# A hybrid diffusion backbone on one core: pads in two tile pools, 64-byte shifts of some weight tiles, and another order inside the attention items

## The chip, the cores and the metric

The kernel runs on one core of one Trainium2 chip. The metric is the device time of one execution in microseconds (us); lower is better. The core has a matrix engine (TensorE, PE in the profile; its weight loads are listed as PEld), three engines for elementwise work (VectorE = DVE, ScalarE = ACT, GpSimd = POOL), and queues that start DMA transfers, of which this kernel uses mainly SP's and POOL's. The on-chip memory SBUF has 128 partitions; a tile occupies the same byte range in each of them, so a tile's place is one byte address. Products accumulate in PSUM.

## The reference

Two layers work on 1024 latent tokens (a 16 x 64 grid) and 256 context tokens of width 1024, in float32.

```python
# layer 0: FNet Fourier groups || bidirectional order-2 Hyena
p = u @ w_in                                   # (L, 2048)
y = concat([fourier_mix(p[..., :512]), hyena_mix(p[..., 512:], ...)]) @ w_out
# layer 1: 2-D neighbourhood attention, 16 heads of 64
s_loc = einsum("bcqhd,bicjhd->bhcqij", q_r, k_b) * scale + bias    # masked outside the window
s_ctx = einsum("bcqhd,bjhd->bhcqj", q_r, kc) * scale               # all 256 context keys
p = softmax(concat([s_loc, s_ctx]))
o = p_loc @ v_b + p_ctx @ vc ;  y = o @ w_out
# after each mixer
h = h + g1 * y
h = h + g2 * ((silu(m @ w_gate) * (m @ w_up)) @ w_down)            # m = modulated RMS norm of h
```

Shifts, scales and gates come from adaLN products of a conditioning vector; the context tokens share all weights, have their own modulation, and need no output in the last layer. The result is the final RMS norm of the latent tokens.

## The kernel before

**Precision and products.** Activations are held transposed, 128 channels on the partitions and tokens along the row. Float32 precision is had from the faster type float32r by splitting: a value is the sum of a high part (a rounded copy, made on ACT by line 280) and a low part (the difference, made on DVE by line 282), and a product is three matmuls, high x high, high x low and low x high. So most of the 16,320 matmuls have float32r operands and move 512 or 256 columns: 512 for each half of the latent tokens, 256 for the context.

**Pools of tiles.** A pool has a number of buffers for each tag, and the pools lie in SBUF in the order in which they are opened: constants (`cp`), wide tiles `s4` (20 of 4096 bytes), `s2` (35 of 2048), `g` (4 of 2048), `pt` (6 `t` tiles of 2048 bytes, and small statistics tiles `ah` and `st` of 32 and 64 bytes, 6 each), `tk` (4 of 2048), and `pw` with the tags `ws`, `wh` and `wl` (2 each of 4096). The profile prints `s4` and `s2` both as `s`. A weight block is loaded by DMA into `ws` (or a wide `s` tile) as float32 and split into `wh` and `wl`; matrices that come as float16 are loaded into `ws` (printed `cs`) and copied to a float32r tile `mat`, which takes buffers of `wh` and `wl` in turn. Activations lie in `s` tiles. In SBUF the last byte used before the change is 227,616 in each partition.

**Stages, in order of time.** Filter spectra of the Hyena branch (to about 210 us), the input projection with the Fourier channel side and the context's filters between its blocks (to about 500), the Hyena convolutions and the Fourier sequence side (to about 780), the output projection, the feed-forward block of layer 0 (context columns first, then gate and up of the latent tokens by a Strassen-Winograd scheme of seven products, line 1246, then down, line 1413, then the context's down, line 1516, to about 1690), the value projection (to about 1870), attention (to about 2330), the rest of the attention's output projection, and layer 1's feed-forward block.

**Roles of the tiles in a matmul.** In the input, output, key, query, gate and up products the weights (`wh`, `wl`) are the stationary operand and an `s` tile moves. In the filter spectra and the forward transforms of the Hyena branch `mat` is stationary. In the inverse Hyena transforms `mat` moves, 256 columns at a time; in the value projection `wh` and `wl` move, 512 at a time. In the later Strassen-Winograd products and in the latent down products both operands are `s` tiles (or `t`).

**Attention.** There are 64 items, one for each head, half of the rows, and pair of column chunks (`attn_item`). An item has three stages: (a) TensorE computes the context scores of both chunks into one PSUM tile and the local scores into two; (b) DVE takes the row maxima (line 1699 for the context, line 1701 for bias plus local scores of each chunk), their negation (1703), ACT takes the exponentials (1706 for the local scores in the `g` tile, 1707 for the context scores in `t`), each with a sum, TensorE transposes the three probability tiles through the identity (1715), ACT copies each to float16 (1718) and DVE makes the low half (1719); (c) TensorE multiplies with the values, and ACT scales the result (1745). Two items of neighbouring stages are in flight, and the key and query projections of the next pair of heads, and at the end the output projection's first part, are issued between the stages as filler.

**Order of the work.** Each engine has its own queue and executes it in order. The code is written in one order; a planner that estimates times then orders each engine's queue, so an edit can move instructions that it doesn't touch.

Of the kernel before, what the change touches and what calls it, by code (L numbers as in the profile page):

```python
# [18 lines left out]
P = 128  # L19
# [4 lines left out]
NFB = 22  # L24
# [6 lines left out]
KSTART = (0, 8, 24, 32)  # L31
BOPS = ("B11", "B21", "T2", "T1", "T3", "B22", "T4")
# [167 lines left out]
class Builder:  # L200
    def __init__(self, ctx, tc, a, out, taps=None, stop=None):
        self.tc, self.nc, self.a, self.out = tc, tc.nc, a, out
        self.taps, self.stop = taps, stop
        ent = ctx.enter_context
        self.cp = ent(tc.tile_pool(name="cp", bufs=1))
        self.p4 = ent(tc.tile_pool(name="p4", bufs=20))
        self.p2 = ent(tc.tile_pool(name="p2", bufs=35))
        self.pg = ent(tc.tile_pool(name="pg", bufs=4))
        self.pt = ent(tc.tile_pool(name="pt", bufs=6))
        self.pko = ent(tc.tile_pool(name="pk", bufs=4))  # L210
        self.pw = ent(tc.tile_pool(name="pw", bufs=2))
        self.pp = ent(tc.tile_pool(name="pp", bufs=6, space=bass.MemoryType.PSUM))
        self.pq = ent(tc.tile_pool(name="pq", bufs=2, space=bass.MemoryType.PSUM))
        self.dr = ent(tc.tile_pool(name="dr", bufs=1, space=bass.MemoryType.DRAM))
        self.k = self.mk = self.pk = 0
        self.banks = 8
        self.sq = {}

# [67 lines left out]

    def pair3(self):

        self.p3 = (getattr(self, "p3", 0) + 1) % 3
        return self.pair2(("ws", "ws") if self.p3 == 0 else ("wh", "wl"))  # L290

    def weights(self, src, w=1024, cut=False, keep=None, wide=False, load=None):
        st = self.S4() if wide else self.pw.tile([P, 1024], F32, tag="ws", name=self.nm("ws"))
        if keep:
            hi, lo = keep
        else:
            hi, lo = self.pair3() if wide == 3 else self.pair2()
        (load or self.ld)(st.rearrange("p (n k) -> p n k", n=4) if cut else st[:, :w], src)
        self.split(st[:, :w], hi[:, :w], lo[:, :w])
        return hi, lo  # L300
# [5 lines left out]
    def cmat(self, w, src, view=None, small=False):  # L306
# [8 lines left out]
        m = self.mat(w)  # L315
# [506 lines left out]
    def hy_inverse(self, sq, o, y):  # L822
# [8 lines left out]
        for h in range(H // hw):  # L831
# [25 lines left out]
            for part, fi, i, fb in mats:  # L857
                ms[(i, fb)] = self.cmat(min(nb, 2) * 512, a["vi_" + sq][h, i, :, fb:fb + min(nb, 2)],
                                        lambda t: t.rearrange("p (f c) -> p f c", c=512), False)
                if sq == "l":  # L860
                    for cb in range(4):
                        product(part, fi, i, fb, cb)
                    yield
# [427 lines left out]
    def ffn(self, l, u, h, hs, second, after, keep=None, begun={}):  # L1291
# [21 lines left out]
        todo = iter(())  # L1313
        if u is not None:
            for fb in range(NFB):
                wide = 3 if fb < NFB - 2 else True
# [77 lines left out]
    def down(self, l, bops, sops, hidc, hs, h, todo, after, keep):  # L1394
# [98 lines left out]
        if l == 0:  # L1493
# [4 lines left out]
            for kb in range(NFB):  # L1498
# [9 lines left out]
                wh, wl = self.pair2()  # L1508
# [165 lines left out]
    def attn_item(self, head, hd, hf, c0, qs, kk, kc, vt, osb, out):  # L1674
# [24 lines left out]
        nc.vector.tensor_reduce(cm, pctx.rearrange("p (i k) -> p i k", i=2), axis=AX, op=MAX)  # L1699
        for i in (0, 1):  # L1700
            nc.vector.tensor_tensor_reduce(bias[i], loc[i][:, :384], bias[i], 1.0, cm[:, i:i + 1], ADD, MAX,
                                           mx[:, i:i + 1])
        nc.vector.tensor_scalar(nm, mx, -1.0, None, op0=MUL)
        pc = self.T()
        for i in (0, 1):
            nc.scalar.activation(bias[i], bias[i], AF.Exp, bias=nm[:, i:i + 1], accum_out=s1[:, i:i + 1])
            nc.scalar.activation(pc[:, i * 256:i * 256 + 256], pctx[:, i * 256:i * 256 + 256], AF.Exp,
                                 bias=nm[:, i:i + 1], accum_out=s2[:, i:i + 1])
        nc.vector.tensor_tensor(s1, s1, s2, ADD)
        nc.vector.reciprocal(rv, s1)  # L1710
        pts = []
        for src, n in ((pc, 4), (bias[0], 3), (bias[1], 3)):
# [7 lines left out]
            pts.append(t)  # L1720
# [437 lines left out]
```

## Time and profile before

| | before |
|---|---|
| median of 3 runs | 3058.11 us (3051.83 to 3061.61) |
| profiled execution | 3055.81 us, of it span 3054.0 us |
| granted TensorE clock, mean | 0.985 |
| PE busy | 2919.6 us (96%), 16,320 matmuls |
| DVE busy | 2076.6 us (68%) |
| ACT busy | 1390.4 us (46%) |
| POOL busy | 460.3 us (15%) |
| DMA | 549.87 MB, mean 180 GB/s |

The span runs from the first to the last instruction; busy times are shares of it. A row of a group reads: line, engine, operation, output tile <- input tiles, shape, number of instructions, then busy time, mean time of one in ns, and the idle time of the engine ahead of them with what ended it. Matmuls are pipelined, so the mean of one is longer than the distance between two starts. A row of the timeline begins with the start and the duration in us of a merged run of instructions. A row of waits names who waited for whom, the total in us, how often, and the longest.

### The profile page before, as it was taken

What the parts mean: (1) busy time and instruction counts of PE and PEld (TensorE: products, weight loads), DVE (VectorE), ACT (ScalarE), POOL (GpSimd) and SP (SyncE); (2) the same over time, 40 slices, a digit from 0 to 9 for tenths busy, and PEclk for the clock granted to TensorE, in tenths of its full rate; (3) what the DMA queues carried; (4) which work ended last, traced back from release to release, by engine and by line L of the source; (5) the groups of instructions that cost most, each with busy time, mean ns of one, the idle gap of its engine ahead of it and who ended that gap; (6) DMA issues with size and microseconds to landing.
All of it is one profiled execution on the core that took longest, in us unless ns stands there. A gap on an engine that the chain in (4) does not pass through costs nothing. (4 is left out here: it accounts for less than half of the span.)

```text
span 3054.0 us, 45753 instructions
## 1 busy us (share of the span) xinstructions
PE 2919.6 (96%) x16320; PEld 2420.3 (79%) x16320; DVE 2076.6 (68%) x3924; ACT 1390.4 (46%) x2581; POOL 460.3 (15%) x751
## 2 busy tenths in 40 slices
PE   7899999999999999999999999999889999999997
PEld 2678888888899788787778888888777788887886
DVE  5767785775677777866677437777676977664545
ACT  4663225453454333333445336777675533333433
POOL 1012012451101111212010000110111022112000
PEclk9999999999999999999999999999999999999999
DMA  6564545466555454659874334454555266535663
GB/s 250 190 204 169 182 141 155 124 199 206 210 172 200 170 181 170 215 177 325 299 252 165 131 126 116 127 143 124 164 180 187 97 234 221 173 111 175 214 193 131
DMA packets 263486, 549.87 MB, mean 180 GB/s; under 512 B 33878, under 2 KB 85784, under 8 KB 263258
## 3 DMA queue, kind: packets, MB, share of 16 engines
q1 hardware_dynamic: 209658, 381.23, 38.5%
q0 software_dynamic: 51296, 161.52, 15.1%
q10 hardware_dynamic: 2304, 4.20, 0.4%
q8 instruction: 128, 2.10, 0.3%
q14 instruction: 100, 0.82, 0.1%
HBM read 418.63 MB, written 119.80 MB: 176 GB/s over the span
## 5 line engine op out<-in xcount | busy, mean ns | idle before, releaser
L1246 PE MATMUL ps<-s,s 128*128 128x512 f32 x2028 | 513.0, 395 | 14.3 <-ACT g L1251 11.0
L1246 PEld LDWEIGHTS ps<-s,s 128*128 128x128 f32 x2028 | 384.6, 190 | 103.4 <-ACT g L1251 13.4
L276 PE MATMUL ps<-s,wh 128*128 128x256 f32 (+1 forms) x1768 | 391.7, 327 | 1.3 <-ACT wh L280 1.3
L276 PEld LDWEIGHTS ps<-s,wh 128*128 128x128 f32 x1768 | 291.4, 188 | 37.2 <-ACT wh L280 3.4
L276 PE MATMUL pq<-s,wh 128*128 128x512 f32 (+1 forms) x984 | 300.9, 384 | 10.3 <-DVE s L1630 7.6
L280 ACT CAST wh<-ws 128x1024 fp32r<-128x1024 f32 (+1 forms) x139 | 142.6, 1026 | 351.2 <-PE ps L276 163.2
L1413 PE MATMUL ps<-s,s 128*128 128x512 f32 (+1 forms) x1000 | 258.6, 384 | 11.2 <-DVE s L282 11.0
L282 DVE TENSOR_TENSOR wl<-ws,wh 128x1024 fp32r<-128x1024 f32 (+1 forms) x139 | 165.7, 1192 | 142.2 <-ACT wh L280 137.3
L280 ACT CAST s<-s 128x1024 fp32r<-128x1024 f32 (+2 forms) x188 | 171.7, 942 | 197.9 <-DMA s<-d 160.1
L276 PE MATMUL ps<-s,wl 128*128 128x256 f32 (+1 forms) x884 | 255.1, 326 | 1.1 <-DVE wl L282 1.1
L276 PE MATMUL ps<-s,s 128*128 128x64 f16 (+3 forms) x2663 | 216.5, 233 | 16.2 <-DVE s L1719 5.9
L1413 PEld LDWEIGHTS ps<-s,s 128*128 128x128 f32 x1000 | 183.7, 188 | 53.0 <-DVE s L282 17.1
L282 DVE TENSOR_TENSOR s<-s,s 128x1024 fp32r<-128x1024 f32 (+2 forms) x166 | 190.7, 1184 | 45.4 <-ACT s L280 44.8
L280 ACT CAST s<-t 128x512 fp32r<-128x512 f32 (+2 forms) x250 | 140.4, 579 | 175.6 <-DVE t L1225 67.6
L276 PEld LDWEIGHTS pq<-s,wh 128*128 128x128 f32 x984 | 177.8, 190 | 45.9 <-DVE s L1630 9.9
L282 DVE TENSOR_TENSOR s<-t,s 128x512 fp32r<-128x512 f32 (+2 forms) x250 | 164.4, 671 | 58.6 <-ACT s L280 32.9
L1246 PE MATMUL ps<-s,wh 128*128 128x512 f32 x608 | 194.9, 398 | 2.0 <-DVE g L1337 2.0
L276 PE MATMUL ps<-s,mat 128*128 128x512 f32 x684 | 180.9, 410 | 6.2 <-ACT s L280 3.2
L276 PE MATMUL pq<-s,wl 128*128 128x512 f32 (+1 forms) x492 | 183.0, 381 | 0.0
L276 PEld LDWEIGHTS ps<-s,wl 128*128 128x128 f32 x884 | 162.1, 188 | 18.5 <-DVE wl L282 1.7
L316 ACT CAST mat<-cs 128x1024 fp32r<-128x1024 f16 (+2 forms) x120 | 111.7, 935 | 131.6 <-PE ps L276 52.4
L276 PEld LDWEIGHTS ps<-s,mat 128*128 128x128 f32 x684 | 132.0, 196 | 43.6 <-DVE s L282 5.4
(379 smaller groups left out, 5666.0 us busy)
## 6 DMA issues: line engine op xcount, KB each, us to landing
s<-d SPq DMA_DIRECT2D x286, 256.0 KB, 3.6
s<-in_down SPq DMA_DIRECT2D x154, 256.0 KB, 4.0
d<-s POOLq DMA_DIRECT2D x137, 256.0 KB, 3.6
d<-tk POOLq DMA_DIRECT2D x98, 256.0 KB, 3.7
s<-in_ada_w POOLq DMA_DIRECT2D x48, 512.0 KB, 4.7
g<-in_bias SPq DMA_DIRECT2D x128, 192.0 KB, 2.9
ws<-in_up SPq DMA_DIRECT2D x44, 512.0 KB, 3.5
d<-g POOLq DMA_DIRECT2D x87, 256.0 KB, 3.3
```

The lines of the kernel that those rows point to most:

```text
L276: self.nc.tensor.matmul(o, l, r, start=st, stop=sp)
L280: self.last_hi = nc.scalar.copy(hi, src).ins
L282: self.last_lo = eng.tensor_tensor(lo, src, hi.bitcast(F32), SUB).ins
L316: self.nc.scalar.copy(m, st)
L1246: nc.tensor.matmul(ps, x[:, sl], y, start=first and j == 0 and x is wh and y is xh, stop=j == 3 and x is wl, skip_group_check=True)
L1413: m = nc.tensor.matmul(acc[j][:, c0:c1], x[:, sl], y[:, xs], start=first and k == 0, stop=last and k == 2, skip_group_check=True)
```

## The change

Two pads are added: 72 float32 columns (288 bytes) in the constants' pool, and 112 columns (448 bytes) in `pt`; each is written once by a memset on POOL. A helper `shifted` takes a tile of 1056 columns in `wh`, `wl` or `ws` and hands out the part that begins 16 columns (64 bytes) in; the context's gate, up and down weights and the matrices of the inverse Hyena transforms (`cmat` with `shift`) are taken through it. The buffers of `wh`, `wl` and `ws` thereby grow from 4096 to 4224 bytes, and the last byte used is 229,120. In an attention item the negated maximum is taken separately for each chunk, right behind that chunk's maximum; the context exponential is issued ahead of the local one; and the transposes go in the order local chunk 0, context, local chunk 1, where the context had been first. In the built queues nothing else is moved ahead of attention or behind it; inside attention all queues have another order.

```diff
+PAD_C, PAD_T, SHIFT = 72, 112, 16
...
+        self.pad(self.cp, PAD_C)
...
+    def pad(self, pool, w):
+
+        self.nc.gpsimd.memset(pool.tile([P, w], F32, name="pad", tag="pad", bufs=1), 0.0)
...
+    def shifted(self, tag, name, w=1024):
+
+        return self.pw.tile([P, 1056], F32R, tag=tag, name=self.nm(name))[:, SHIFT:SHIFT + w]
+
+    def pair1(self):
+        return self.shifted("wh", "wh"), self.shifted("wl", "wl")
+
     def pair3(self):
 
         self.p3 = (getattr(self, "p3", 0) + 1) % 3
-        return self.pair2(("ws", "ws") if self.p3 == 0 else ("wh", "wl"))
+        tags = ("ws", "ws") if self.p3 == 0 else ("wh", "wl")
+        return [self.shifted(g, n) for g, n in zip(tags, ("wh", "wl"))]
...
-            hi, lo = self.pair3() if wide == 3 else self.pair2()
+            hi, lo = self.pair3() if wide == 3 else self.pair1() if wide == 2 else self.pair2()
...
-        m = self.mat(w)
+        if shift:
+            self.mk ^= 1
+            m = self.shifted(("wh", "wl")[self.mk], "mat", w)
+        else:
+            m = self.mat(w)
...
-                                        lambda t: t.rearrange("p (f c) -> p f c", c=512), False)
+                                        lambda t: t.rearrange("p (f c) -> p f c", c=512), False, True)
...
+        if l == 0:
+            self.pad(self.pt, PAD_T)
...
-                wide = 3 if fb < NFB - 2 else True
+                wide = 3 if fb < NFB - 2 else 2
...
-                wh, wl = self.pair2()
+                wh, wl = self.pair1()
...
         nc.vector.tensor_reduce(cm, pctx.rearrange("p (i k) -> p i k", i=2), axis=AX, op=MAX)
+        pc = self.T()
         for i in (0, 1):
             nc.vector.tensor_tensor_reduce(bias[i], loc[i][:, :384], bias[i], 1.0, cm[:, i:i + 1], ADD, MAX,
                                            mx[:, i:i + 1])
-        nc.vector.tensor_scalar(nm, mx, -1.0, None, op0=MUL)
-        pc = self.T()
-        for i in (0, 1):
-            nc.scalar.activation(bias[i], bias[i], AF.Exp, bias=nm[:, i:i + 1], accum_out=s1[:, i:i + 1])
+            nc.vector.tensor_scalar(nm[:, i:i + 1], mx[:, i:i + 1], -1.0, None, op0=MUL)
             nc.scalar.activation(pc[:, i * 256:i * 256 + 256], pctx[:, i * 256:i * 256 + 256], AF.Exp,
                                  bias=nm[:, i:i + 1], accum_out=s2[:, i:i + 1])
+            nc.scalar.activation(bias[i], bias[i], AF.Exp, bias=nm[:, i:i + 1], accum_out=s1[:, i:i + 1])
...
-        for src, n in ((pc, 4), (bias[0], 3), (bias[1], 3)):
+        for k, src, n in ((1, bias[0], 3), (0, pc, 4), (2, bias[1], 3)):
...
-            pts.append(t)
+            pts[k] = t
```

More of the change, by code (lines that the diff above doesn't have):

```diff
@@ L304, in mat, with cmat @@
         return self.pw.tile([P, w], dt, tag=("wh", "wl")[self.mk], name=self.nm("mat"))
-    def cmat(self, w, src, view=None, small=False):
+    def cmat(self, w, src, view=None, small=False, shift=False):
         if small:
@@ L1702, in attn_item @@
                                            mx[:, i:i + 1])
-        nc.vector.tensor_scalar(nm, mx, -1.0, None, op0=MUL)
-        pc = self.T()
-        for i in (0, 1):
-            nc.scalar.activation(bias[i], bias[i], AF.Exp, bias=nm[:, i:i + 1], accum_out=s1[:, i:i + 1])
+            nc.vector.tensor_scalar(nm[:, i:i + 1], mx[:, i:i + 1], -1.0, None, op0=MUL)
             nc.scalar.activation(pc[:, i * 256:i * 256 + 256], pctx[:, i * 256:i * 256 + 256], AF.Exp,
                                  bias=nm[:, i:i + 1], accum_out=s2[:, i:i + 1])
+            nc.scalar.activation(bias[i], bias[i], AF.Exp, bias=nm[:, i:i + 1], accum_out=s1[:, i:i + 1])
         nc.vector.tensor_tensor(s1, s1, s2, ADD)
         nc.vector.reciprocal(rv, s1)
-        pts = []
-        for src, n in ((pc, 4), (bias[0], 3), (bias[1], 3)):
+        pts = [None] * 3
+        for k, src, n in ((1, bias[0], 3), (0, pc, 4), (2, bias[1], 3)):
             ps = self.PS()
```

## Prediction

> **What bounds the kernel now.** I read the page first, then busy time by stage, then the timeline of TensorE inside long back-to-back runs, and last the waits of the attention stage.
>
> ```profile
> span 3054.0 us, 45753 instructions
> ...
> PE 2919.6 (96%) x16320; PEld 2420.3 (79%) x16320; DVE 2076.6 (68%) x3924; ACT 1390.4 (46%) x2581; POOL 460.3 (15%) x751
> ...
> PEclk9999999999999999999999999999999999999999
> ```
>
> TensorE is busy for 2919.6 of 3054.0 us at a clock that is never below 0.9, and no other engine passes 68%. So time can come out of this kernel in two ways: each matmul takes less, or the remaining 134 us of TensorE idle time shrink. The next view, busy time in four stretches, says where each way is open (columns: stretch, length, then busy us of PE, PEld, DVE, ACT, POOL, clock, DMA share, GB/s).
>
> ```profile
> 0.00:100.00 100.00, 81.80 (x257) 38.63 (x258) 47.20 (x84) 43.86 (x75) 10.55 (x24) 0.97 0.65 230
> 100.00:200.00 100.00, 89.94 (x365) 67.47 (x364) 81.63 (x130) 80.14 (x116) 1.06 (x2) 0.93 0.63 208
> 1870.00:2330.00 460.00, 424.80 (x3933) 362.30 (x3932) 332.38 (x812) 318.62 (x924) 61.75 (x116) 0.99 0.51 151
> 2500.00:2800.00 300.00, 300.00 (x1311) 245.75 (x1309) 191.47 (x289) 101.85 (x165) 52.45 (x98) 1.00 0.47 160
> ```
>
> From 2500 to 2800 us (layer 1's gate and up products) TensorE never stops: there a shorter matmul is a shorter kernel, one for one. In attention (1870 to 2330) 35.2 us are idle. Only the first 200 us wait a lot for other things (28.3 us idle).
>
> **What one matmul costs, by its two addresses.** The page's mean durations of a matmul overlap its neighbours, so I take the distance between starts in runs without a gap.
>
> ```profile
> 1126.05 0.63 PE L1246 MATMUL ps<-s,wh 128*128 128x512 f32 x2
> ...
> 1131.64 8.35 PE L1246 MATMUL ps<-s,s 128*128 128x512 f32 x36
> 1139.83 0.40 PE L1246 MATMUL ps<-s,wh 128*128 128x512 f32 x1
> ```
> ```profile
> 625.22 6.54 PE L276 MATMUL ps<-s,mat 128*128 128x512 f32 x27
> 631.60 0.86 PE L276 MATMUL pq<-s,mat 128*128 128x512 f32 x3
> ```
> ```profile
> 835.81 0.40 PE L276 MATMUL ps<-s,wh 128*128 128x256 f32 x2
> ...
> 840.92 0.50 PE L276 MATMUL pq<-c,tk 128*128 128x1 f32 x4
> ```
> ```profile
> 3024.17 0.64 PE L1413 MATMUL ps<-s 128*128 128x256 f32 x4
> ...
> 3029.95 0.39 PE L1413 MATMUL ps<-s 128*128 128x256 f32 x1
> ```
>
> Of 512 columns: 24 matmuls with weights in wh/wl take 5.59 us (232.9 ns each), and the 36 that follow on the same line with weights in s tiles take 8.19 us (227.5 ns). With weights in mat: 27 in 6.38 us (236.3 ns). Of 256 columns the order is reversed: 45 with weights in wh/wl take 5.11 us (113.6 ns), 48 with both operands in s tiles 5.78 us (120.4 ns). So it isn't that wh/wl is slow memory. What fits both signs is where the two operands stand to each other. The pools give the addresses: the constants end at byte 20192, which is 96 modulo 128, and the pools of s, g and t follow in multiples of 128; pt's small tiles then add 6 x 32 + 6 x 64 = 576 bytes, 64 modulo 128. So s, g and t lie at 96 and wh, wl, ws, mat at 32: a pair (s, s) has distance 0 modulo 128, a pair (s, wh) 64. Distance 0 is the quick one at 512 columns, distance 64 at 256.
>
> **The change, part by part.** PAD_C (288 bytes) lifts every pool from 96 to 0 modulo 128, and PAD_T (448) cancels the 576, so wh, wl and ws come to 0 as well. SHIFT then puts 64 bytes back for some 256-column users: the context's gate, up and down (pair1, pair3) and the inverse Hyena matrices. In the built program all 512-column float32r pairs of both kinds come to distance 0.
>
> (1) Their number, by groups of the view by line and form:
>
> ```profile
> L276 PE MATMUL pq<-s,wh 128*128 128x512 f32 x824 | 273.5, 404 | 10.3 <-DVE s L1630 7.6 <-DVE s L1990 1.4 <-DVE s L1617 1.0
> ...
> L276 PE MATMUL ps<-s,wh 128*128 128x512 f32 x712 | 237.1, 399 | 0.7 <-ACT wh L280 0.7
> ...
> L1246 PE MATMUL ps<-s,wh 128*128 128x512 f32 x608 | 194.9, 398 | 2.0 <-DVE g L1337 2.0
> ...
> L276 PE MATMUL ps<-s,mat 128*128 128x512 f32 x684 | 180.9, 410 | 6.2 <-ACT s L280 3.2 <-DVE s L282 3.0
> ```
>
> With their six smaller companions of the same lines (wl, and the pq accumulators: 412, 356, 304, 132, 96 and 48) they are 4176. Each goes from 232.9 to 227.5 ns: 4176 x 5.4 = 22.6 us less. The mat group could give 8.8 instead of 5.4; I keep 5.4 for all and leave 816 x 3.4 = 2.8 us to the range.
>
> (2) The value projection has the roles exchanged (moving operand in wh/wl, 480 matmuls by the code). Between nothing and 5.4 ns each, 0 to 2.6 us; nearest is the lower end, since the distance is the same but another operand is off: I take 0.8 us less.
>
> (3) Unshifted 256-column users lose: the context columns of w_in (16 blocks of 24), w_out (8 of 24) and wk (8 of 24), 768 matmuls, go from distance 64 to 0: 768 x 6.8 = 5.2 us more (lower end 0, as they stand between 512-column ones).
>
> (4) The first 200 us don't follow TensorE alone: I drop the gain of one latent filter spectrum, 4 x 4 x 4 x 3 = 192 matmuls, 1.0 us.
>
> Position in all: 22.6 + 0.8 - 5.2 - 1.0 = 17.2 us less. The gain spreads over stages with DVE at most at 82% (the second stretch above), so I name no new bound; in 2500 to 2800 DVE stays at 191 of 300 us, and that cover would be gone only with matmuls a third shorter.
>
> (5) The order inside an attention item. The built order of all queues, SP's and POOL's included, is the same as before ahead of attention and behind it; inside, the planner has moved TensorE's projection matmuls between the items, and the bias loads on SP go with their items. These rows are of 1870 to 2330 us:
>
> ```profile
> PE ps L1715 <- ACT t L1707: 10.3, 13, 1.7
> PE pq L276 <- DVE s L1630: 7.6, 7, 4.6
> PE ps L276 <- DVE s L1719: 5.9, 10, 1.0
> ```
> ```profile
> L1706 ACT ACTIVATE g<-g,st 128x384 f32<-128x384 f32 x120 | 74.3, 619 | 33.0 <-DVE st L1703 29.8 <-DVE st L1709 1.5 <-DVE st L1710 1.2
> L1707 ACT ACTIVATE t<-ps,st 128x256 f32<-128x256 f32 x120 | 56.3, 469 | 0.1
> ...
> L1707 ACT ACTIVATION_READ_ACCUMULATOR t<-ps,st 128x1 f32 x120 | 24.5, 204 | 0.0
> ```
> ```profile
> L1701 DVE CUSTOM_DVE_ANT_0 g<-ps,g,st 128x384 f32<-128x384 f32 x119 | 70.7, 614 | 46.0 <-PE ps L276 31.1 <-DMA g<-in_bias 10.2 <-PE ps L1715 2.1
> ...
> L1699 DVE TENSOR_REDUCE st<-ps 128x2 f32<-128x512 f32 x59 | 40.5, 686 | 21.3 <-PE ps L276 20.9
> ...
> L1703 DVE TENSOR_SCALAR st<-st 128x2 f32<-128x2 f32 x60 | 10.0, 166 | 1.0
> ```
>
> Before, the first transposes of an item read the context exponentials, of which the second is the last of four on ACT. What has to end ahead of it: row maximum 0.69, two bias maxima 2 x 0.61, negation 0.17, then two exponentials of 0.62 and two of 0.47 with their read-outs (four of about 0.2), 5.1 us without hand-overs. In the built order the TensorE work between an item's last score matmul and its first transpose, priced by the starts above, is 2.7 us at least and under 4.4 us for a quarter of the 64 items; hence the 13 waits of 10.3 us. After, the first transposes read bias 0, ready after 0.69 + 0.61 + 0.17 + 0.47 + 0.62 and two read-outs, 3.0 us, under a cover of 3.1 us at least. The context group then needs 3.7 us under 3.5 (a tenth of the items under 3.8), the last one 4.5 under 3.9 (a tenth under 5.0). So nearly all of the wait goes; I take 9.0 of the 10.3 us. The added instruction (one negation per group, 64 more of 0.17 us, 10.6 us on DVE) lies beside 127 us of DVE idle time. Queued behind it on DVE is the second bias maximum, which is needed only by the last group. What is late next are the 7.6 us behind the query split (L1630) and the 5.9 us behind the transposes' low halves (L1719), which I leave. Bounds: at best all 35.2 us of idle go, at worst the 10.6 us come onto the path.
>
> (6) The two memsets on POOL (72 and 112 columns) cost nothing: POOL is busy 460 of 3054 us, and nobody reads the pads. Transfers keep their sizes.
>
> **The sum.** 17.2 + 9.0 = 26.2 us less in the profiled execution: 3054.0 becomes 3027.8. That execution took 3055.81 us with 1.8 us around the span, and the median of the runs, 3058.11, lies 2.3 us above it; kept so, 3031.9, and I say 3032.
>
> **Rivals.**
>
> *The distance does nothing.* The slower pace would then belong to how wh, wl and mat are made or used; (1) to (4) vanish and only attention gains: 3058 - 9 = 3049. Against it stands the change of sign: 113.6 against 120.4 ns at 256 columns, 232.9 against 227.5 at 512, with the same kinds of tile. [...]
>
> *Not the distance but the place counts (slower than before).* Every quick 512-column pair of this trace starts at 96 modulo 128, none at 0. If 0 itself is a bad start, the place is every (s, s) pair too: 4624 matmuls by the built program. At 232.9 ns they cost 4624 x 5.4 = 25.0 us, the 22.6 and 0.8 don't come, and the 5.2 may still be paid: 25.0 + 5.2 - 9.0 = 21 us more, 3079. Today's mean over the 9280 pairs is (4176 x 232.9 + 480 x 229.2 + 4624 x 227.5) / 9280 = 230.0 ns (229.2 being 227.5 + 0.8 / 480); above some 230.4 at the new place the kernel is slower. Against it: the moving operand starts at 96 in all of the runs quoted, quick and slow, so its start alone doesn't set the pace.
>
> *Attention gives nothing back.* Its reordered projections wait elsewhere, most likely for L1630, whose longest wait is already 4.6 us, or the negation's 10.6 us come onto the path. Then 3041 to 3052.
>
> *Position gives all it can.* Add 2.8 and 1.8 us, drop the 5.2, and half of attention's idle time goes, 17.6 us: 17.2 + 9.8 + 17.6 = 44.6, 3013.
>
> **How the numbers follow.** About 0.3% (9 us) is what a measurement here can tell from no change. My forecast's case (3020 to 3041) has 0.60, position's best case with it 0.10, attention without a gain 0.10, no effect of distance 0.12, the bad start 0.06, something else 0.02. The time is that of the likeliest, 3032. The range runs from the best case, 3012, to 3053, which takes in the third rival and the second end of the first, and leaves out the bad start. Faster: 0.60 + 0.10 + 0.09 of the third rival, and 0.02 of the first, which ends at the border: 0.81. Same: 0.12; slower: 0.07.
>
> **What would show it.** In the new profile the timeline of a gate and up product should show its 24 matmuls with weights in wh/wl at 227 to 228 ns between starts, where they were at 232.9, and the 36 behind them unchanged; 300 us inside those products should hold about 1320 matmuls, not 1311 (the 381 with weights in wh or wl 5.4 ns shorter each). The context products of 256 columns should stay at 113.6. Attention's wait of L1715 for L1707 should fall from 10.3 to about 1 us and its idle time from 35 to about 26. The prediction is wrong if (s, s) pairs change their pace, if (s, wh) pairs keep theirs, or if attention's idle time grows.

## The result and the profile after

| | before | after |
|---|---|---|
| median | 3057.2 us (8 runs, 3051.83 to 3064.67) | 3044.9 us (8 runs, 3041.55 to 3059.69) |
| ratio after / before | | 0.9963 (0.9947 to 0.9980) |
| profiled execution | 3055.81 us, span 3054.0 | 3045.79 us, span 3044.0 |
| granted TensorE clock | 0.985 | 0.985 |

The kernel became faster by 12.3 us, where 25 to 26 had been forecast; the time lies inside the range given, but the gain is half of the one that was worked out. It also lies in the range of the rival "attention gives nothing back" (3041 to 3052), and not for that rival's reason: the positions gave half of their term too. The page of the kernel after (engine, busy us, share, instructions):

```profile
span 3044.0 us, 45809 instructions
...
PE 2907.4 (96%) x16320; PEld 2420.9 (80%) x16320; DVE 2078.8 (68%) x3988; ACT 1392.5 (46%) x2581; POOL 461.5 (15%) x753
```

TensorE is busy for 12.2 us less with the same 16,320 matmuls, and DVE has the 64 added negations. Nothing else of note moved on the page, so two questions remain: why the matmuls gave less than 4176 x 5.4 us, and what happened to the 9 us of attention.

The first is answered by the timeline of the very product that the prediction quotes (layer 0, gate and up; start, duration, instructions), and by its counterpart in layer 1, both of the kernel after. Line 1246 has become line 1264.

```profile
1121.53 0.64 PE L1264 MATMUL ps<-s,wh 128*128 128x512 f32 x2
...
1127.12 8.33 PE L1264 MATMUL ps<-s,s 128*128 128x512 f32 x36
...
1135.29 0.62 PE L1264 MATMUL ps<-s,wh 128*128 128x512 f32 x2
...
2490.50 0.62 PE L1264 MATMUL ps<-s,wh 128*128 128x512 f32 x2
...
2495.94 2.88 PE L1264 MATMUL pq<-s,s 128*128 128x512 f32 x12
```

In layer 0 the 24 matmuls with weights in wh and wl still take 5.59 us, 232.9 ns each, to the digit what they took before, though their distance is 0 modulo 128 now. In layer 1 another 24 of the same form take 5.44 us, 226.7 ns. So the change works for some blocks of weights and not at all for others. The addresses of the built program say which: `shifted` makes the buffers of `wh`, `wl` and `ws` 4224 bytes long, 33 x 128, so the second buffer of each tag lies 128 bytes off a multiple of 256 (wl at 203,776 and 208,000, wh at 212,224 and 216,448), while all buffers of the `s`, `g` and `t` tiles lie at multiples of 256. Of the 9280 float32r pairs of 512 columns 6938 are at distance 0 modulo 256 and 2342 at 128. The slow run reads a buffer of the second kind, the quick one of the first.

For attention, busy time by stretch and TensorE's waits (us in total, times, longest) in the kernel after:

```profile
1870.00:2330.00 460.00, 427.83 (x3928) 367.34 (x3928) 335.03 (x866) 319.11 (x915) 66.26 (x124) 0.99 0.50 154
```
```profile
PE ps L282 <- DVE st L1722: 12.9, 14, 3.1
PE ps L1734 <- DVE s L1738: 4.6, 8, 0.7
PE ps L1734 <- DVE st L1722: 3.3, 3, 1.1
PE pq L282 <- DVE s L2009: 2.8, 1, 2.8
...
PE ps L1734 <- ACT g L1727: 1.2, 3, 0.6
```

The transposes (now line 1734) wait 1.2 us for an exponential instead of 10.3, and the 7.6 us behind the query split are gone as well. But 460.00 - 427.83 = 32.2 us are idle, 3.0 less than before and not 9: at the head stands a wait of 12.9 us for the bias maxima (line 1722, 1701 before). Before, this wait was

```profile
PE ps L276 <- DVE st L1701: 4.2, 8, 0.9
```

### The profile page after: what moved, and what is told of

It reads as the page before. It is cut to its first block, busy times and chain, and to the rows that moved or that the text cites. A ratio compares the mean times of both kernels' runs of the same rounds, so it can differ in the third digit from the quotient of the medians.

```text
span 3044.0 us, 45809 instructions
## 1 busy us (share of the span) xinstructions
PE 2907.4 (96%) x16320; PEld 2420.9 (80%) x16320; DVE 2078.8 (68%) x3988; ACT 1392.5 (46%) x2581; POOL 461.5 (15%) x753
## 4 chain that ended last, share of the span: by engine, by line
PE 37%; issue 16%; DVE 6%; DMA 5%; POOL 2%; ACT 1%; SPq 0%; POOLq 0%; DVEq 0%; ACTq 0%
PE ps L1264 10%; PE pq L282 8%; PE ps L282 7%; PE ps L1433 4%; PE pq L1264 3%; PE ps L1536 2%; DMA s<-d 1%; PE ps L1734 1%; PE pq L1433 1%; POOL d L273 1%; DVE s L288 1%; DMA g<-in_bias 1%; DMA ws<-in_up 1%; DMA s<-in_ada_w 1%; DMA ws<-in_gate 0%
## 5 line engine op out<-in xcount | busy, mean ns | idle before, releaser
L282 PE MATMUL ps<-s,s 128*128 128x64 f16 (+3 forms) x2663 | 216.1, 233 | 23.8 <-DVE st L1722 12.9
```

Of the source, the lines that this page charges most:

```text
L282: self.nc.tensor.matmul(o, l, r, start=st, stop=sp)
```

## The experiments

Each time is the median of a kernel; its ratio is to the kernel before in runs on the same chip, with a 95% interval. The runs fall into three sets on three chips, in which the kernel before took 3056.55 us (`e1` to `e4`), 3054.26 us (`e5` to `e8`) and 3058.47 us (`e9` to `e11`), so across sets the ratios are to be compared. "Distance" is that of the two operands' start addresses. A pace is the time between the starts of neighbouring matmuls of one run.

**Each half alone.** `e1_positions` is the kernel after with the old attention item:

```diff
-            nc.vector.tensor_scalar(nm[:, i:i + 1], mx[:, i:i + 1], -1.0, None, op0=MUL)
+        nc.vector.tensor_scalar(nm, mx, -1.0, None, op0=MUL)
+        pc = self.T()
+        for i in (0, 1):
+            nc.scalar.activation(bias[i], bias[i], AF.Exp, bias=nm[:, i:i + 1], accum_out=s1[:, i:i + 1])
             nc.scalar.activation(pc[:, i * 256:i * 256 + 256], pctx[:, i * 256:i * 256 + 256], AF.Exp,
                                  bias=nm[:, i:i + 1], accum_out=s2[:, i:i + 1])
-            nc.scalar.activation(bias[i], bias[i], AF.Exp, bias=nm[:, i:i + 1], accum_out=s1[:, i:i + 1])
...
-        for k, src, n in ((1, bias[0], 3), (0, pc, 4), (2, bias[1], 3)):
+        for src, n in ((pc, 4), (bias[0], 3), (bias[1], 3)):
```

> The changed kernel with the old attention item: pads, shifts and wider buffers alone. The built addresses say that with buffers of 4224 bytes every second wh, wl and mat buffer lies 128 bytes off modulo 256 from the s tiles: of the 9280 512-column pairs 6938 are at distance 0 modulo 256 and 2342 at 128. Theory 'period 256': quick is distance 0 modulo 256 only; 2314 of the 4656 pairs that were to gain do gain 5.4 to 6 ns and 2342 stay slow, so the positions alone give 6 to 9 us, 3048 to 3051 us, with runs of matmuls at 227 and runs at 232 to 238 ns beside each other. Rival 'period 128, and the rest of the slow pace belongs to the wh and wl tiles': the same time here, but the pace would not follow the buffer. Rival 'the gain came from attention': 3055 to 3058.

`e2_attention` is the kernel before with the new item alone, the reverse of that diff:

```diff
+            nc.vector.tensor_scalar(nm[:, i:i + 1], mx[:, i:i + 1], -1.0, None, op0=MUL)
...
-        for src, n in ((pc, 4), (bias[0], 3), (bias[1], 3)):
+        for k, src, n in ((1, bias[0], 3), (0, pc, 4), (2, bias[1], 3)):
```

> The kernel before with the new order inside the attention items alone; all addresses as before. The two traces show a lead of 5.4 us when attention begins and 10.0 at the end, so the order is worth 2 to 4 us by that: 3053 to 3055. By the prediction's step it would be worth 9 us: 3048. If the new wait of the score matmuls for the maxima (12.3 us in the changed kernel) costs as much as the old wait for the exponentials (10.3) saved: 3057.

Measured: positions alone 3048.08 us, ratio 0.9969 (0.9957 to 0.9982); order alone 3051.09 us, ratio 0.9983 (0.9970 to 0.9996); the kernel before had 3056.55. So the positions are worth 8.5 us and the order 5.5 us, where 17.2 and 9.0 had been forecast. Both terms came out at about half, with the right sign; the order lies between the cases that its expectation names (3053 to 3055, and 3048). Attention in `e2_attention` (stretch, then TensorE's longest wait and the next) shows that the longer wait belongs to the order, not to the addresses:

```profile
1870.00:2330.00 460.00, 429.49 (x3963) 368.82 (x3962) 337.67 (x878) 323.72 (x929) 64.97 (x122) 0.99 0.50 152
```
```profile
PE ps L276 <- DVE st L1702: 11.7, 11, 2.6
PE ps L1714 <- DVE s L1718: 4.5, 8, 0.6
```

Idle time there is 30.5 us, 4.7 less than before, close to the 5.5 us gained.

**All buffers at distance 0.** `e3_slots4352` is the kernel after with `wh` and `wl` buffers of 4352 bytes (17 x 256) and the pads made to fit, so that all 9280 pairs are at 0 modulo 256:

```diff
-PAD_C, PAD_T, SHIFT = 72, 112, 16
+PAD_C, PAD_T, SHIFT = 8, 48, 16
...
-        return self.pw.tile([P, 1056], F32R, tag=tag, name=self.nm(name))[:, SHIFT:SHIFT + w]
+        return self.pw.tile([P, 1056 if tag == "ws" else 1088], F32R, tag=tag, name=self.nm(name))[:, SHIFT:SHIFT + w]
```

> The changed kernel with wh and wl buffers of 4352 bytes (17 x 256) in place of 4224 (33 x 128), and pads of 8 and 48 columns in place of 72 and 112 to make room: all 9280 512-column pairs then stand at distance 0 modulo 256, the shifted 256-column ones at 64 or 192 as before. Theory 'period 256': the 2342 pairs at 128 go from 233 to 238 ns to 227, 14 to 20 us less than the changed kernel, 3026 to 3032 us, and no (s, wh) run shows more than 228. Rival 'period 128, the rest belongs to wh and wl': no change from the changed kernel, 3045.

`e8_dist128` is `e3_slots4352` with a pad that puts 4656 pairs, those with an operand in `wh`, `wl` or `mat`, at 128 modulo 256, which is still 0 modulo 128:

```diff
-PAD_C, PAD_T, SHIFT = 8, 48, 16
+PAD_C, PAD_T, SHIFT = 8, 80, 16
```

> The kernel with 4352-byte buffers and the pad behind the small tiles grown by 128 bytes, so that all (s, wh), (s, mat) and (wh, s) pairs of 512 columns stand at distance 128 modulo 256 (4656 of them) and the (s, s) pairs at 0. Theory 'period 256': every gate and up run with weights in wh and wl at about 233 ns, the inverse of e3_slots4352 where all were at 227; 3700 pairs outside mixed runs at some 6 ns, 18 to 24 us above e3_slots4352: 3055 to 3064, at or above the kernel before. Rival 'period 128': 3039 as in e3_slots4352.

The same product of layer 0 in the timeline of `e3_slots4352`, then of `e8_dist128`:

```profile
1118.58 0.62 PE L1264 MATMUL ps<-s,wh 128*128 128x512 f32 x2
...
1124.02 8.32 PE L1264 MATMUL ps<-s,s 128*128 128x512 f32 x36
```
```profile
1125.17 0.64 PE L1264 MATMUL ps<-s,wh 128*128 128x512 f32 x2
...
1130.76 8.34 PE L1264 MATMUL ps<-s,s 128*128 128x512 f32 x36
```

24 matmuls take 5.44 us (226.7 ns) at distance 0 and 5.59 us (232.9 ns) at 128. The times follow: 3039.11 us, ratio 0.9943 (0.9927 to 0.9960), against 3050.05 us, ratio 0.9989 (0.9973 to 1.0004). One pad of 128 bytes costs 11 us by the medians and 14 by the ratios (18 to 24 had been expected), and at distance 128 hardly anything is left of the gain. So 128 bytes aren't a period, and 256 fits the three distances tried at 512 columns: 226.7 ns at 0, 232.9 at 64 (the kernel before) and 232.9 at 128. But `e3_slots4352` had been expected at 3026 to 3032; it came only 5.8 us below the kernel after (3044.9; the two intervals overlap) and 12.0 us below the order alone (3051.09). So the period isn't the whole answer.

**Does the place count?** `e5_place64` is `e3_slots4352` with 64 bytes more in the first pad: all distances stay, every tile starts at 64 modulo 256.

```diff
-PAD_C, PAD_T, SHIFT = 8, 48, 16
+PAD_C, PAD_T, SHIFT = 24, 48, 16
```

> The kernel with 4352-byte buffers (e3_slots4352, 3039 us), all pools moved up by another 64 bytes: every distance is as there, every place is 64 instead of 0 modulo 256. Theory 'distance': no change, 3036 to 3042, 227 ns in the gate and up products. Rival 'place' (the prediction's slow case, a start at which both operands are slow): 232 ns or more in (s, s) pairs too, 3060 to 3080.

```profile
1130.15 0.62 PE L1264 MATMUL ps<-s,wh 128*128 128x512 f32 x2
...
1135.59 8.32 PE L1264 MATMUL ps<-s,s 128*128 128x512 f32 x36
```

Again 5.44 us for 24; 3041.45 us, ratio 0.9959 (0.9944 to 0.9974), whose interval overlaps that of `e3_slots4352`. At 512 columns the distance counts (226.7 ns at 0 against 232.9 at 128); of the place, 0 or 64, nothing is seen.

**The shift.** `e4_noshift` is the kernel after without the 64 bytes and with buffers of 4096, so that everything, the context's 256-column products too, is at distance 0:

```diff
-        return self.pw.tile([P, 1056], F32R, tag=tag, name=self.nm(name))[:, SHIFT:SHIFT + w]
+        return self.pw.tile([P, 1024], F32R, tag=tag, name=self.nm(name))[:, :w]
```

> The changed kernel without the 64-byte shifts, buffers back at 4096 bytes, pads kept: every pair, of 512 and of 256 columns, stands at distance 0 modulo 256. Theory 'period 256': 512 columns as in the run with 4352-byte buffers (227 ns), but 2448 matmuls of 256 columns go from about 114 or 117 to 119 to 120 ns, 8 to 15 us more than that run: 3036 to 3046. Rival 'period 128': 512 columns as slow as in the changed kernel and 256 columns slower, 3053 to 3060.

3044.54 us, ratio 0.9957 (0.9943 to 0.9971): the same as the kernel after. It gains the full pace at 512 columns (24 matmuls of a gate and up product, from 1126.13 us on, take 5.44 us, 226.7 ns each) and pays it back at 256, as one run of context products shows:

```profile
831.52 0.40 PE L282 MATMUL ps<-s,wh 128*128 128x256 f32 x2
...
836.79 0.28 PE L282 MATMUL ps<-s,wh 128*128 128x256 f32 x1
```

44 matmuls take 5.27 us, 119.8 ns each, and all unbroken runs of context products in this trace take 119.2 to 120.0. Away from distance 0 there isn't one pace but two, some 113.5 and some 117.8 ns, and the distance doesn't decide between them. Here are the same context products at the same distances, 54 matmuls from the first row to the second, in `e3_slots4352` and then in `e5_place64`:

```profile
850.78 0.40 PE L282 MATMUL ps<-s,wh 128*128 128x256 f32 x2
...
856.90 0.39 PE L282 MATMUL ps<-s,wh 128*128 128x256 f32 x2
```
```profile
855.06 0.40 PE L282 MATMUL ps<-s,wh 128*128 128x256 f32 x2
...
861.43 0.40 PE L282 MATMUL ps<-s,wh 128*128 128x256 f32 x2
```

6.12 us are 113.3 ns each, 6.37 us are 118.0, and both runs keep their pace for some 885 matmuls. It isn't the place either: `e7_transposes_only`, whose tiles lie where those of `e3_slots4352` do, takes 118.1 there. The kernel before has both paces as well: 113.6 ns in the 45 matmuls that the prediction quotes, 117.8 in the 36 from 841.93 us on, both at distance 64. What decides isn't known. So by the paces the shift is worth 2 to 6.5 ns a matmul; by the times, `e4_noshift` is 5.4 us above `e3_slots4352`, with intervals that overlap. What the shift cost in the kernel after is the odd buffer length.

**Where the rest of the positions' gain went.** `e3_slots4352` has all pairs at 0 and is still 6 us dearer than expected. Its traces and those of the kernel before differ in what they gain by kind of run (ns between starts, means over the unbroken pairs of the traces):

| 512-column pairs | number | before (64) | distance 0 | distance 128 |
|---|---|---|---|---|
| gate and up, weights in wh/wl | 1056 | 233.3 | 226.8 | 232.8 to 233.1 |
| weights in mat | 816 | 233.2 | 227.9 | 232.4 to 232.7 |
| key projection | 384 | 233.2 | 228.2 | 232.5 |
| value projection, wh/wl moving (before: 64 the other way round) | 480 | 228.9 | 226.8 | 232.4 |
| input and output projection, mixed with 256-column ones | 960 | see below | see below | |
| query projection, moving operand in pieces of 16 columns | 384 | 237.3 | 238.6 to 239.2 | 238.9 |
| attention's output projection, in pieces as well | 384 | 236.5 | 231.8 to 233.7 | 235.7 |

The mixed runs issue a 256-column matmul and one or two of 512 columns on the same weights. In the timeline each row here begins one such triple of the input projection, 18 triples apart, first in the kernel before, then in `e3_slots4352`:

```profile
341.69 0.51 PE L276 MATMUL ps<-s,wh 128*128 128x256 f32 x2
...
352.13 0.51 PE L276 MATMUL ps<-s,wh 128*128 128x256 f32 x2
```
```profile
339.84 0.51 PE L282 MATMUL ps<-s,wl 128*128 128x256 f32 x2
...
350.39 0.51 PE L282 MATMUL ps<-s,wl 128*128 128x256 f32 x2
```

10.44 / 18 = 580.0 ns before, 10.55 / 18 = 586.1 ns at distance 0 in this block; over all unbroken triples (some 290 of the 384) the means are 580.3 and 586.2, and over the unbroken pairs of the output projection (256 and 512 columns, 176 of 192) 353.3 and 353.4. (The 583.7 of the next expectation is not what the trace gives.) So 960 of the 4176 pairs give nothing, the triples lose a little. `e9_widths_apart` (which also has the single negation of `e6_one_negation`, below) issues all 256-column matmuls of a weight block first and the 512-column ones after them; `e10_before_apart` does that alone to the kernel before:

```diff
-        for i, kb in enumerate(ks):
+        runs = [r for r in ([p for p in pcs if WID[p] == 256], [p for p in pcs if WID[p] == 512]) if r]
+        for run, i, kb in ((r, i, kb) for r in runs for i, kb in enumerate(ks)):
...
-                for pc in pcs:
+                for pc in run:
```

> e6_one_negation (4352-byte buffers, one negation, 3037.5 us) with the input and output projections' matmuls put in another order: for each weight block all 256-column ones of the context first, then all 512-column ones, instead of one after the other on the same weights. In the traces a triple of 256, 512 and 512 columns takes 580.7 ns at distance 64 and 583.7 at distance 0, so those pairs had no gain; apart, by the paces of unmixed runs, it should take 119.5 + 2 x 227 = 573.5 ns. 384 triples x 10 and 192 pairs of 256 and 512 x 10: 5 to 6 us less, 3030 to 3034. If the mixed runs are slow for another reason: no change, 3036 to 3039.

> The kernel before with the same reordering alone, all distances as before (64). Unmixed at distance 64 a triple costs 114 + 2 x 233.3 = 580.6 ns, mixed 580.7: no change, 3053 to 3059. If the reordering helps by itself (evictions of the context columns earlier, for one): 3048 to 3053.

The 512-column part of one block of the input projection in `e9_widths_apart`:

```profile
343.51 0.40 PE L282 MATMUL pq<-s,wh 128*128 128x512 f32 x1
...
352.36 0.39 PE L282 MATMUL ps<-s,wl 128*128 128x512 f32 x1
```

39 matmuls take 8.85 us, 226.9 ns each; with a 256-column one at 119.8 (above) that is 573.7 ns for the work of a triple, 12.5 less than the mean of the mixed ones. 384 x 12.5 ns and 6.7 for each of the 192 pairs (353.4 - 119.8 - 226.9) make 6.1 us. The 1000 matmuls from the 1000th on, which hold most of the input projection, take 189.7 us in this trace, 194.1 in that of `e6_one_negation` and 192.1 in the kernel before. Its time is 3030.16 us, ratio 0.9909 (0.9888 to 0.9930), the lowest of all kernels here; `e6_one_negation` has 3037.50 us and 0.9949 (0.9936 to 0.9963) on another chip. That is 7.3 us by the medians and 12 by the ratios, more than the paces give; where the rest comes from is open. On the kernel before the same reordering gives 3061.59 us, ratio 1.0016 (0.9998 to 1.0033), above the 3053 to 3059 expected but no change by the ratio, as the paces say: 113.6 + 2 x 233 = 580, what a mixed triple takes there. So the order of the widths was worth something at distance 0 (7.3 us by the medians) and nothing that these runs show at 64 (ratio 1.0016). Why a mixed run doesn't profit isn't settled; nothing in the trace shows what the matmuls in it stand behind.

The pairs of the last two rows of the table read their moving operand through a permuted view. `e11_contiguous` is `e6_one_negation` with that view left out, so that the columns, and with them the result, come out in another order:

```diff
-            return x.rearrange("p (r h c) -> p h r c", r=8, h=4)
+            return x
...
-            return x.rearrange("p (h r c) -> p r h c", r=8, h=4)
+            return x
```

> e6_one_negation with the query projection and the attention's output projection moving their 512 columns in the order in which they lie, not in pieces of 16 columns (it leaves out that permutation, so the columns come out in another order). In the traces those 768 matmuls keep 233 to 236 ns at distance 0 while unbroken ones take 228. If the pieces are the reason, they go to 227 to 229 ns and the time to 3030 to 3034; if attention's other traffic is, they stay, 3036 to 3040.

A query projection in the kernel before, in `e6_one_negation` and in `e11_contiguous`; the second row begins 15 matmuls behind the first:

```profile
1856.82 0.64 PE L276 MATMUL pq<-s,wh 128*128 128x512 f32 x2
...
1860.38 0.64 PE L276 MATMUL pq<-s,wh 128*128 128x512 f32 x2
```
```profile
1848.84 0.65 PE L282 MATMUL pq<-s,wh 128*128 128x512 f32 x2
...
1852.44 0.65 PE L282 MATMUL pq<-s,wh 128*128 128x512 f32 x2
```
```profile
1851.03 0.62 PE L282 MATMUL pq<-s,wh 128*128 128x512 f32 x2
...
1854.45 0.61 PE L282 MATMUL pq<-s,wh 128*128 128x512 f32 x2
```

15 matmuls take 3.56 us (237.3 ns each) before, 3.60 us (240.0) at distance 0, and 3.42 us (228.0) at distance 0 in one piece: the pieces of 16 columns are what kept the query's pairs slow. But the time is 3039.85 us, ratio 0.9938 (0.9915 to 0.9961), no better than `e6_one_negation` (0.9949). The expected time didn't come, and why is open. Most of these pairs are filler between attention items, so longer waits may have taken the gain; that is not shown. The granted clock may have taken it as well: the four executions of `e11_contiguous` had 0.980 to 0.984, the six of `e6_one_negation` 0.982 to 0.986, and of the kernel before, on the chip of `e11_contiguous`, one execution took 3066.05 us at 0.982 and another 3047.64 us at 0.988.

**Attention.** `e6_one_negation` is `e3_slots4352` with one negation for both chunks, behind the second maximum, and the exponentials and transposes in the new order; `e7_transposes_only` is `e3_slots4352` with maxima, negation and exponentials in the old order and only the transposes in the new one.

```diff
-            nc.vector.tensor_scalar(nm[:, i:i + 1], mx[:, i:i + 1], -1.0, None, op0=MUL)
+        nc.vector.tensor_scalar(nm, mx, -1.0, None, op0=MUL)
+        for i in (0, 1):
             nc.scalar.activation(pc[:, i * 256:i * 256 + 256], pctx[:, i * 256:i * 256 + 256], AF.Exp,
```

> e3_slots4352 with one negation behind both maxima again, all else of the new item order kept (context exponential first, transposes local 0, context, local 1). In e3_slots4352 the value products wait 12.1 us for the second maximum (L1722), whose PSUM bank they take over. If that wait comes from the negation between the two maxima on DVE, it falls to about 4 to 8 us and the time by 3 to 6, to 3033 to 3036; if it comes from the order in which TensorE arrives, it stays at 11 to 13 us and the time at 3037 to 3041, or rises by 1 to 3 as the first exponential starts 0.7 us later.

```diff
-            nc.vector.tensor_scalar(nm[:, i:i + 1], mx[:, i:i + 1], -1.0, None, op0=MUL)
+        nc.vector.tensor_scalar(nm, mx, -1.0, None, op0=MUL)
+        pc = self.T()
+        for i in (0, 1):
+            nc.scalar.activation(bias[i], bias[i], AF.Exp, bias=nm[:, i:i + 1], accum_out=s1[:, i:i + 1])
             nc.scalar.activation(pc[:, i * 256:i * 256 + 256], pctx[:, i * 256:i * 256 + 256], AF.Exp,
                                  bias=nm[:, i:i + 1], accum_out=s2[:, i:i + 1])
-            nc.scalar.activation(bias[i], bias[i], AF.Exp, bias=nm[:, i:i + 1], accum_out=s1[:, i:i + 1])
```

> e3_slots4352 with the old order of maxima, negation and exponentials, and only the transposes reordered (local 0, context, local 1). If the gain of the new item order is in the transposes, the wait of L1734 for the exponentials stays small for the first group, and the time at 3037 to 3041; if it is in the early exponentials, TensorE waits for the context exponentials in the second group, 5 to 8 us in all, and the time is 3042 to 3046.

3037.50 us, ratio 0.9949 (0.9936 to 0.9963), and 3045.50 us, ratio 0.9975 (0.9964 to 0.9986). TensorE's waits for the bias maxima and for the low halves in attention of `e3_slots4352`, then of `e6_one_negation`, then its waits for the maxima in `e7_transposes_only`, and a stretch of `e6_one_negation` and of `e11_contiguous`:

```profile
PE ps L282 <- DVE st L1722: 12.1, 11, 3.2
PE ps L1734 <- DVE s L1738: 4.6, 8, 0.7
PE ps L1734 <- DVE st L1722: 3.2, 3, 1.1
```
```profile
PE ps L1735 <- DVE st L1722: 6.0, 5, 3.3
PE ps L1735 <- DVE s L1739: 4.7, 8, 1.4
PE ps L282 <- DVE s L1739: 4.2, 9, 1.2
PE ps L282 <- DVE st L1722: 4.2, 7, 0.9
```
```profile
PE ps L282 <- DVE st L1721: 11.0, 12, 2.9
PE ps L1735 <- DVE st L1721: 6.0, 6, 1.9
```
```profile
1838.00:2320.00 482.00, 450.13 (x4136) 387.74 (x4136) 354.29 (x859) 339.86 (x978) 68.19 (x128) 0.99 0.50 154
```
```profile
1838.00:2320.00 482.00, 449.40 (x4134) 390.44 (x4133) 351.68 (x856) 340.01 (x983) 66.52 (x125) 0.98 0.49 150
```

With one negation the value products (line 282) wait 4.2 us for the maxima, as before the change, instead of 12.1. But this doesn't show that the negation between the maxima made the wait: `e7_transposes_only` has one negation behind both as well, and there they wait 11.0 us. Nor does it save time. The transposes' wait for the maxima rises from 3.2 to 6.0 in `e6_one_negation`, and the two times can't be told apart, so the fall of the wait came as expected and the time didn't. What sets this wait is open; when TensorE arrives at it is the rival that the expectation of `e6_one_negation` names.

Of the new order the early exponentials, together with the transposes, are what pays. From the first local score product to the last value product the traces take

| kernel | order of the item | us | of it TensorE idle |
|---|---|---|---|
| before | old | 485.7 | 36.8 |
| `e1_positions` | old | 484.0 | 36.7 |
| `e7_transposes_only` | only the transposes new | 483.7 | 36.0 |
| `e2_attention` | new | 478.7 | 32.9 |
| `e3_slots4352` | new | 475.6 | 32.0 |
| `e6_one_negation` | new, one negation | 475.6 | 31.9 |

The transposes alone bring nothing, and the gain over the kernel before sinks from the 0.9949 of `e6_one_negation` to 0.9975. The time of `e7_transposes_only` is as expected, the mechanism isn't: TensorE's waits for the context exponentials were to be 5 to 8 us and are 3.8 in its trace. The stretches of `e6_one_negation` and `e11_contiguous` hold as many matmuls (4136 and 4134) and as much idle time (31.9 and 32.6 us), at a granted clock of 0.99 and 0.98.

## Why the prediction was wrong, point by point

*What bounds the kernel.* Right outside attention: a shorter matmul was a shorter kernel. The 300 us of layer 1's gate and up products, moved with the lead, hold 1318 matmuls and no idle time, where 1311 had been and about 1320 forecast; `e5_place64`, with all pairs at 0, has 1325 there, and `e8_dist128`, with those in wh and wl at 128, has 1311:

```profile
2490.00:2790.00 300.00, 300.00 (x1318) 247.18 (x1318) 193.08 (x293) 103.52 (x169) 52.67 (x99) 1.00 0.47 163
```

Inside attention TensorE waits for DVE and ACT as well (32.2 us idle in the kernel after), and taking a wait away there moved part of it to the next one, as step (5) tells.

*Step (1), 22.6 us: failed.* Two parts of it were wrong. "All 512-column float32r pairs come to distance 0" was reckoned modulo 128, from paces at the distances 0 and 64 alone, which can't tell a period of 128 from one of 256; modulo 256 half of the affected pairs came to 128, which is as slow as 64 (232.9 ns). And 5.4 ns was carried from unbroken runs of one width to all 4176 pairs. The 960 in mixed runs lose at distance 0 (5.9 ns a triple, nothing a pair: 2.3 us), and of the 768 with a moving operand in pieces the 384 of the query lose 1 to 2 each and the other 384 give 3 to 5; only 2448 are outside these, and those that were measured give 5.0 to 6.5. Half of 2448 at 6 ns is 7.3 us, near the 8.5 of `e1_positions`. With all at 0, 2448 x 6 = 14.7 us, about 1 of the value projection and 1 of the pieces, less 2.3 us for the mixed runs and 1 for the 192 matmuls of the key's context columns at some 5 ns, are about 13; 12.0 separate `e3_slots4352` from `e2_attention`. The 236.3 ns for weights in mat, from which the 2.8 us of the range came, is a misreading: the first of the 27 distances, behind a short matmul, is 317 ns, and the other 26 are 233.3. Some of the rest may be in TensorE's wait for ACT in the gate and up products, 11.0 us in the kernel before and 16.9 in `e3_slots4352`, by its waits over the whole span,

```profile
PE ps L1264 <- ACT g L1269: 16.9, 8, 4.3
```

but `e6_one_negation`, with the same addresses, has 11.9 there, so this wait isn't tied to the distance and was left open.

*Step (2), the value projection: wrong in the kernel after.* At distance 0 it gives 2.1 ns each, near the 1.7 assumed (0.8 us over 480), but half of it was put at 128, where it costs 3.5 ns more than before (232.4, by `e8_dist128`).

*Step (3), 256 columns: right in sign, one pace where there are two.* The loss at distance 0 is there (119.8 ns), and in the triples it comes together with the 512-column ones' missing gain. But 6.8 ns is its upper end: the price of distance 64 was taken from one run at 113.6, and other runs of the same kernel at the same distance take 117.8. The key's context columns went from a mean of 117.0 to 121.6. The forecast that the shifted context products stay at 113.6 has the same flaw: in the kernel after the longest run takes 113.8 ns over 885 matmuls and shorter ones 115.4 to 118.3, and the kernel before has both paces too.

*Step (4), the first 200 us.* A term of 1.0 us is below what the runs can separate; nothing was tried on it.

*Step (5), 9.0 us: half right.* The wait of the transposes for the exponentials fell from 10.3 to 1.2 as forecast, and the query split's went with it. What failed is to take 9.0 of those 10.3 us as time won, with the query split and the low halves as what is late next, and with it the sentence "queued behind it on DVE is the second bias maximum, which is needed only by the last group". The maximum is also the last reader of the local scores in PSUM, and value products wait for it:

```profile
L282 PE MATMUL ps<-s,s 128*128 128x64 f16 x1920 | 67.8, 194 | 14.1 <-DVE st L1722 12.9 <-ACT s L1737 0.9 <-DVE s L1738 0.3
```

That they wait is in the row. That it is for the PSUM buffer follows from the built program: in 63 of the 64 items the value products write a buffer that this line was the last to read (in 56 before the change). So 10.3 + 7.6 us of waits went and 8.7 came (4.2 to 12.9) with some smaller ones, and idle time fell by 3.0 us in the profile, 4.7 with the order alone. Why this wait grew stays open: the added negation isn't enough to explain it, since it is 11.0 us in `e7_transposes_only`, which has no added one.

*Step (6), the memsets:* no sign of them in the time.

*The rivals.* "The distance does nothing" is refuted by `e3_slots4352` and `e8_dist128`, 11 us apart by one pad of 128 bytes: the same instructions on the same data take 226.7 and 232.9 ns. "The place counts" is refuted by `e5_place64` for the places 0 and 64. "Attention gives nothing back" named a wait elsewhere, for L1630, or the negation on the path. Half of the gain did go to a wait elsewhere, but to the one for the bias maxima; L1630's wait went away, and taking the added negation out again (`e6_one_negation`) gave no time.

## What to carry to other kernels

Before a pace measured in one kind of run is multiplied by a count, split the count by what surrounds each instruction (same width as its neighbours or not, operand in one piece or not) and measure each part. Measure it in more than one run, too: one and the same distance gave 113.6 and 117.8 ns here. Two distances don't give a period: when tile addresses matter, work out the address of every buffer of a tag, since one odd buffer length puts every second one elsewhere. Before a wait that is taken away is counted as time won, look for what the engine waits for next, and ask of a late instruction not only who needs its result but whose buffer it is the last to read.

## What the runs showed of the hardware

Every figure here is of this kernel and its variants, at a mean granted clock of 0.98 to 0.99; a pace is the time between two starts in an unbroken run of float32r matmuls, a distance is that of the start addresses of the two operands, modulo 256 bytes.

- 512 columns, gate and up products with weights in wh/wl: 226.7 ns at distance 0, with both operands' place at 0 (`e3_slots4352`) and at 64 (`e5_place64`); 232.9 at 64 (the kernel before) and 232.9 at 128 (`e8_dist128`). With weights in mat 233.2 at 64 and 227.9 at 0, in the key projection 233.2 and 228.2.
- The value projection, where the two kinds of tile have changed roles: 228.9 ns in the kernel before (64 the other way round), 226.8 at 0, 232.4 at 128.
- 256 columns, weights in wh/wl: 119.2 to 120.0 ns at distance 0 (`e4_noshift`). At 64 the kernel before has runs of 113.6 and of 117.8; the kernel after, with distances of 64 and 192, has 113.8 over 885 matmuls and 115.4 to 118.3 in shorter runs. What decides is open.
- Both widths mixed on the same weights: a triple of the input projection took 580.0 ns at 64 (the kernel before) and 586.1 at 0 (`e3_slots4352`), and 573.7 at 0 with the widths apart (`e9_widths_apart`), by the sum of its paces.
- The query projection, with a moving operand in pieces of 16 columns: 237.3 ns at 64 (the kernel before), 240.0 at 0 (`e6_one_negation`), 228.0 at 0 in one piece (`e11_contiguous`).
- Plain float32, 512 columns: six products of the kernel before, from 34.37 us on, left two records each, 429 ns between starts, so some 858 ns a product.
- TensorE's 16,320 matmul records came in the order of its queue in the built program, line by line, in the kernel before and in the kernel after.

What makes these paces, no run shows.
